# The first modulation woven into the convolution's products, the second layer's last gate summed a layer earlier, and bias tiles loaded beside its attention

## The chip, the cores and the metric

The kernel runs on one core of a Trainium2 chip. The core has five engines that run their own instruction streams: TensorE (PE in the profile, with its weight loads apart as PEld), VectorE (DVE), ScalarE (ACT), GpSimd (POOL) and SyncE (SP), which here issues all loads, one after the other, to the core's 16 DMA engines. The engines wait for each other only where an instruction needs something that another one makes, and each takes its instructions in the order in which they stand in its stream. The metric is the device time of one execution in microseconds, the median of several runs.

## The reference

Two models of two layers each run one after the other on 256 tokens of width 1024, all in 32-bit floats. The change touches the first model, whose layers mix a differential attention, a pooling and a convolution, then run an FFN. Six vectors per layer (`sh1` to `g2`, each 1024 wide) come from a product of a conditioning vector with `w_mod`, and they modulate the norms and gate the sums. The second model's dilated attention adds a bias by relative position.

```python
def adaln(cond, w_mod, b_mod):
    m = jnp.dot(jax.nn.silu(cond), w_mod) + b_mod
    return jnp.split(m[..., None, :], 6, axis=-1)

for l in range(DEPTH):                      # first model, DEPTH = 2
    sh1, sc1, g1, sh2, sc2, g2 = adaln(c, w_mod[l], b_mod[l])
    csh1, csc1, cg1, csh2, csc2, cg2 = adaln(c_ctx, w_mod[l], b_mod[l])
    h = modulate(rms_norm(x, norm1_g[l]), sh1, sc1)          # h * (1 + sc1) + sh1
    hc = modulate(rms_norm(xc, norm1_g[l]), csh1, csc1)
    q, k, v, up, ca, cb = project_inputs(h, w_in[l], ...)    # ca, cb: the convolution's inputs
    ...                                                      # the same for hc (context)
    mix = concatenate([attn, pool_o, conv_o])
    x = x + g1 * (mix @ w_out[l])
    x = x + g2 * swiglu(modulate(rms_norm(x, norm2_g[l]), sh2, sc2), w_ffn_in[l], w_ffn_out[l])
    ...                                                      # layer 0: the same for xc, 512 tokens in all

for l in range(DEPTH):                      # second model
    ...
    o_b = dilated_attention(q_d, k_d, v_d, rel_bias)         # s + bias[t5_bucket(rel)]
    x = x + mixed @ w_out[l]
    x = x + conv_ffn(rmsnorm(x, ffn_norm[l]), w_up[l], conv_w[l], conv_b[l], w_down[l])
```

## The kernel before

Every weight matrix is read from memory once, in pieces of 512 KB. A piece lands in a buffer `raw` (four of them), ScalarE casts it into the high half of a buffer `hl` (L202), VectorE subtracts to get the low half (L204), and a product of 32-bit accuracy is three TensorE matmuls: high with high, high with low, low with high (all through `mm`, L156). A load waits until the VectorE instruction that last read its `raw` buffer is done. All loads are issued by SP in program order (`dma`, L148). Outputs gather in PSUM banks named `acc`, `aux` and `ob`.

**The start** (`start()`). `x` and the context are loaded, normalized and turned by TensorE transposes (`turn`, copies at L768 and L770). The convolution's inputs need the modulated norm: `mod(c)` multiplies the conditioning vector with chunk `c` of `w_mod` (four chunks, buffers `wm` and `a`), and `products(c)` modulates two of the eight blocks of 128 columns of the normalized input, casts and subtracts them (L780, L781), and runs 24 matmuls of 128x512 on the convolution's weights. The program's order is `mod(0)`, `mod(1)`, `products(0)`, `mod(2)`, `products(1)` and so on. Between `products(2)` and `products(3)` SP gets many small loads (parameter `rows`, `gb`, `poolw`, `km`), and two transposes of `rows` (L309) follow all products on TensorE. Then the convolution's gate (`conv_gate`, L1204 and L1205) empties the banks, and `layer1` begins with the query projection (`qk_chunk`, `acc<-hl,a` 128x512).

**The weave.** `weave(main, side, rate)` runs two generators: at each step of the main one the side one is given `rate` steps, and what is left of the side at the end of the main runs after it. In layer 0 the FFN (`ffn_wide`, 512 tokens) is the main and `side2` the side, with rate 0.85. A step of `side2` is, for most of its length, one of `ada_sums`: a load of a `w_mod` block (128x1024) into `raw` and a multiply-add on VectorE (L353 for the first of eight, L355 for the other seven). After eight, `sums_to_gates` (or `sums_to_cols`) sums over partitions with a TensorE product (`aux<-s,ones`) and adds the result to the gate, which was loaded with `b_mod` (L398).

**Layer 1** (256 tokens, `layer1` with `l=1`). First the convolution's inputs (`conv_proj`, four pieces of `w_in`, 24 matmuls of 128x256 each), then query, key, pooling and values woven with the convolution's taps (L1236 on VectorE), then the attention woven with the output projection (`out_proj`, 96 matmuls of 128x512 in all), then the FFN (`ffn_narrow`, 256 tokens: per 256 hidden columns 96 matmuls `aux<-a,hl` 128x256 and 24 `acc<-hl,a` 128x512). The FFN is woven with `side3`: seven empty steps, the eight sums of part 5 of layer 1 (the gate `g2`), `dil_bias` (16 loads of `dbias`, 16x8x256 each, into two tiles for the second model), and `prepare2(0)`, the small loads for the second model's first layer. That model's FFN is woven with a side that has no sums.

The place of each instruction in its engine's stream follows from the program's order and a scheduler that fills in work that was put off (`later`, `flush`, `behind`).

## Time and profile before

| | |
|---|---|
| median of 3 runs | 1668.41 us (1668.08 to 1669.04) |
| the profiled execution | 1668.3 us, of which the span in the trace is 1666.5 us |
| TensorE busy | 1620.5 us, 97% of the span |
| VectorE, ScalarE, GpSimd busy | 1163.9, 793.5 and 40.9 us |
| mean granted TensorE clock | 0.986 of full speed |
| read from memory | 259.84 MB, 157 GB/s over the span |

All times below are microseconds from the start of the span. TensorE is busy nearly throughout, so what counts are the few stretches in which it waits or runs at a reduced clock, and what ends these waits. A busy time of TensorE is modelled from its matmuls' ends.

### The profile page before, as it was taken

Reading aid. Unit: us, or ns where it says so; the run is one execution under the profiler, and the core shown is the slowest. Engines: PE = TensorE matmul, PEld = TensorE weight load, DVE = VectorE, ACT = ScalarE, POOL = GpSimd, SP = SyncE. Lnnn points to the kernel's source line nnn. Section 1 sums busy time; section 2 is a strip of 40 time slices with the busy share of each in tenths; the row PEclk is TensorE's granted clock in tenths of the full one; section 3 lists DMA queues with packets and bytes.
Section 4 is the critical chain, followed back from the end, with each engine's and each line's share of the span. In section 5 each row is a group of like instructions: output and inputs, shape, how many; then the busy total and the mean of one; then the engine's idle time right before and its main releaser. Section 6 shows DMA issues by size and latency. Waiting matters only on the chain.

```text
span 1666.5 us, 24530 instructions
## 1 busy us (share of the span) xinstructions
PE 1620.5 (97%) x9401; PEld 1376.3 (83%) x9401; DVE 1163.9 (70%) x2074; ACT 793.5 (48%) x1339; POOL 40.9 (2%) x99
## 2 busy tenths in 40 slices
PE   7999989999999999999799899999999999999999
PEld 5787568878888888886799798888999888799998
DVE  4796656857575455977565558767887887678786
ACT  4334446323222224555543346755555576665553
POOL 1000000000000000000000001000000010000000
PEclk8999999999999999999899999999999999999999
DMA  9421651745375543532379655423656554246653
GB/s 329 127 91 56 244 181 56 238 150 167 110 233 169 174 149 103 152 112 76 110 224 250 181 184 166 137 88 117 193 187 190 168 161 146 74 130 190 190 181 123
DMA packets 183013, 262.75 MB, mean 158 GB/s; under 512 B 11277, under 2 KB 122864, under 8 KB 182896
## 3 DMA queue, kind: packets, MB, share of 16 engines
q1 hardware_dynamic: 182616, 260.85, 49.9%
q8 instruction: 74, 1.21, 0.3%
q10 hardware_dynamic: 280, 0.33, 0.2%
q14 instruction: 43, 0.35, 0.1%
HBM read 259.84 MB, written 1.31 MB: 157 GB/s over the span
## 4 chain that ended last, share of the span: by engine, by line
PE 83%; DVE 9%; issue 4%; ACT 3%; POOL 1%; DMA 1%; SPq 0%; ACTq 0%; POOLq 0%; DVEq 0%
PE aux L156 40%; PE acc L156 33%; PE ob L156 7%; PE aux L248 3%; DVE hl L204 2%; DVE a L1236 2%; DVE s L1236 1%; ACT hl L202 1%; DMA raw<-in_w_in_dram 1%; ACT s L461 1%; DVE sm L843 1%; POOL sm L163 0%; DVE s L852 0%; DVE a L862 0%; SPq L148 0%
## 5 line engine op out<-in xcount | busy, mean ns | idle before, releaser
L156 PE MATMUL acc<-hl,a 128*128 128x512 f32 (+3 forms) x3072 | 717.4, 387 | 8.3 <-ACT hl L202 2.9
L156 PEld LDWEIGHTS acc<-hl,a 128*128 128x128 f32 x3072 | 554.5, 190 | 117.6 <-ACT hl L202 4.7
L202 ACT CAST hl<-raw 128x1024 fp32r<-128x1024 f32 (+2 forms) x382 | 393.8, 1037 | 474.2 <-PE aux L156 151.2
L156 PE MATMUL aux<-a,hl 128*128 128x256 f32 (+1 forms) x4032 | 578.4, 304 | 4.7 <-ACT hl L202 1.6
L204 DVE TENSOR_TENSOR hl<-raw,hl 128x1024 fp32r<-128x1024 f32 (+2 forms) x382 | 457.3, 1201 | 166.5 <-ACT hl L202 164.5
L156 PEld LDWEIGHTS aux<-a,hl 128*128 128x128 f32 x4032 | 540.0, 192 | 37.4 <-ACT a L462 2.0
L355 DVE SCALAR_TENSOR_TENSOR s<-raw,csf,s 128x1024 f32<-128x1024 f32 x70 | 88.6, 1280 | 45.1 <-DMA raw<-in_w_mod_dram 45.0
L248 PEld LDWEIGHTS aux<-km,s 128*128 128x128 f32 (+1 forms) x416 | 48.9, 144 | 35.0 <-issue 17.6
L248 PE MATMUL aux<-km,s 128*128 128x128 f32 (+1 forms) x416 | 65.8, 283 | 11.9 <-DVE s L443 8.0
L156 PEld LDWEIGHTS ob<-a,s 128*128 128x128 f32 x416 | 52.1, 194 | 15.9 <-ACT s L1313 9.7
L156 PE MATMUL ob<-a,hl 128*128 128x512 f32 (+1 forms) x288 | 64.3, 372 | 0.0
L156 PE MATMUL ob<-a,s 128*128 128x64 f32 (+1 forms) x416 | 56.8, 281 | 2.4 <-ACT s L1313 1.7
L156 PEld LDWEIGHTS ob<-a,hl 128*128 128x128 f32 x288 | 51.2, 188 | 9.3
L524 ACT ACTIVATE s<-aux 128x512 f32<-128x512 f32 x33 | 19.7, 597 | 66.0 <-PE aux L156 66.0
L552 ACT ACTIVATE s<-s,c2a,c2b 128x256 f32<-128x256 f32 x88 | 47.9, 592 | 3.3 <-DVE s L549 3.2
L527 ACT CAST a<-s 128x512 fp32r<-128x512 f32 x33 | 20.4, 618 | 54.7 <-DVE s L526 54.6
L549 DVE TENSOR_TENSOR s<-aux,km 128x512 f32<-128x512 f32 x44 | 30.4, 690 | 20.7 <-PE aux L156 20.7
L1236 DVE SCALAR_TENSOR_TENSOR a<-up,c,a 128x512 f32<-128x512 f32 x60 | 43.3, 743 | 0.5
L248 PE MATMUL aux<-km,a 128*128 128x128 f32 (+1 forms) x196 | 31.9, 295 | 11.0 <-ACT a L770 7.1
L525 DVE SCALAR_TENSOR_TENSOR s<-s,aux 128x512 f32<-128x512 f32 x33 | 22.6, 684 | 28.0 <-ACT s L524 28.0
L409 ACT ACTIVATE jk<-a 128x512 bf16<-128x512 f32 x44 | 28.2, 641 | 26.3 <-DVE a L1023 19.9
L248 PEld LDWEIGHTS aux<-km,a 128*128 128x128 f32 (+1 forms) x196 | 24.0, 148 | 19.3 <-ACT a L770 7.5
(255 smaller groups left out, 1329.3 us busy)
## 6 DMA issues: line engine op xcount, KB each, us to landing
raw<-in_w_ffn_in_dram SPq DMA_DIRECT2D x88, 512.0 KB
raw<-in_w_up_dram SPq DMA_DIRECT2D x88, 512.0 KB
raw<-in_w_in_dram SPq DMA_DIRECT2D x60, 512.0 KB
raw<-in_w_mod_dram SPq DMA_DIRECT2D x56, 512.0 KB
raw<-in_w_ffn_out_dram SPq DMA_DIRECT2D x44, 512.0 KB
raw<-in_w_down_dram SPq DMA_DIRECT2D x44, 512.0 KB
wm<-in_w_mod_dram SPq DMA_DIRECT2D x16, 1024.0 KB
raw<-in_w_out_dram SPq DMA_DIRECT2D x32, 512.0 KB
```

What stands on the lines that cost most here:

```text
L156: self.nc.tensor.matmul(o, lhsT, rhs, start=start, stop=stop)
L202: nc.scalar.copy(hl[:, 0, :n], raw[:, :n])
L204: nc.vector.tensor_sub(hl[:, 1, :n], raw[:, :n], hl[:, 0, :n].bitcast(F32))
L248: self.nc.tensor.transpose(b[:rows, j * P:(j + 1) * P], s, self.ident)
L355: self.nc.vector.scalar_tensor_tensor(accs[s], raw, c, accs[s], op0=ALU.mult, op1=ALU.add)
L409: self.nc.scalar.activation(junk, x[:, h * 512:(h + 1) * 512], AF.Square, scale=D ** -0.5, accum_out=ss[:, h:h + 1])
L524: nc.scalar.activation(th, g, AF.Tanh, scale=0.5)
L525: nc.vector.scalar_tensor_tensor(th, th, 1.0, g, op0=ALU.add, op1=ALU.mult)
L527: nc.scalar.copy(hi, th)
L549: nc.vector.tensor_mul(y, x.rearrange("p (j t) -> p j t", j=2), R2)
L552: nc.scalar.activation(o[:, j, :], y[:, j, :], AF.Identity, scale=wc(1, ff), bias=bc(ff))
L1236: nc.vector.scalar_tensor_tensor(o, up[:, ct, :, k:k + SEQ], w, o, op0=ALU.mult, op1=ALU.add)
```

## The change

It has four parts. In `start()`, `mod(c+1)` now runs inside `products(c)`, after the first of its two blocks; the splits of the weights are held behind its copies, and the first splits of the query weights behind the last cast and subtraction. The sums of layer 1's part 5 move from `side3` to the end of `side2`, so into layer 0's FFN; the gate's load and `sums_to_gates` stand right after `conv_proj` in layer 1. The loads of `dil_bias` move from `side3` to the side of layer 1's attention, one step beside each step of the output projection. With these gone, `prepare2(0)` stands earlier in `side3`.

```diff
-    def split(self, raw, a, b, mark=None):
+    def split(self, raw, a, b, mark=None, first=None):
...
-        nc.scalar.copy(hl[:, 0, :n], raw[:, :n])
+        with self.behind(first):
+            nc.scalar.copy(hl[:, 0, :n], raw[:, :n])
...
-        def mod(c):
+        def mod(c, mark=None):
...
-                for k0 in (0, 4):
-                    self.ada_products(rb[:, o:o + 256], k0, raws[c, part][:, k0:k0 + 4, :])
-                nc.scalar.copy(r[:, o:o + 256], rb[:, o:o + 256])
+                with self.behind(mark):
+                    for k0 in (0, 4):
+                        self.ada_products(rb[:, o:o + 256], k0, raws[c, part][:, k0:k0 + 4, :])
+                copy = nc.scalar.copy(r[:, o:o + 256], rb[:, o:o + 256])
...
+            return end, copy
...
-                        self.mm(o, lo[:, j, w], hT[0][h][:, kk, :], start=False, stop=(k == KD - 1))
+                        mark = self.mm(o, lo[:, j, w], hT[0][h][:, kk, :], start=False, stop=(k == KD - 1))
+                if j == 0 and c < 3:
+                    ends = mod(c + 1, mark)
+            return ends if c < 3 else (sub, cast)
...
-        mod(0)
-        w_split(0)
+        w_split(0, mod(0))
         w_load(1)
         mod_load(2)
-        mod(1)
-        products(0)
-        w_split(1)
+        w_split(1, products(0))
...
-        products(3)
-        first = [self.split(raw, 2, 512) for raw in first]
+        ends = products(3)
+        first = [self.split(raw, 2, 512, *ends) for raw in first]
...
         if last:
+            g2 = [self.gate(l, 5, 0)]
+            self.sums_to_gates(g2)
             band = band_load()
...
                 yield from self.ada_sums(l + 1, 2, [0])
                 self.sums_to_gates([self.gate_next])
+                yield from self.ada_sums(l + 1, 5, [0])
...
-        self.weave(
-            self.diff_attention(S, qT, kT, v, rq, q_toks, mA, LAG), (next(out) for _ in range(4)), 0.5)
+        bias = []
+
+        def side():
+            tables = self.dil_bias(bias)
+            for _ in range(4):
+                next(out)
+                next(tables, None)
+                yield
+
+        self.weave(self.diff_attention(S, qT, kT, v, rq, q_toks, mA, LAG), side(), 0.5)
...
-        g2 = [self.gate(l, 5, 0)]
...
             for _ in range(7):
                 yield
-            yield from self.ada_sums(l, 5, [0])
-            self.sums_to_gates(g2)
-            yield from self.dil_bias(bias)
             nxt.append(self.prepare2(0))
```

**The order on the engines.** The following rows are the instruction streams before and after at three places; a row is line, operation, output and inputs (with buffer numbers), and shape. Lines after L153 are one to nine higher in the changed kernel.

At the boundary of layer 0 and layer 1, SP's stream before: the last `w_mod` blocks of `side2`, then the four pieces of `conv_proj`, then the first piece of the query weights.

```order
L148 DMA raw_5201<-in_w_mod_dram 128x1024
L148 DMA raw_5204<-in_w_mod_dram 128x1024
L148 DMA raw_5219<-in_w_in_dram 128x8x128
L148 DMA raw_5272<-in_w_in_dram 128x8x128
L148 DMA raw_5306<-in_w_in_dram 128x8x128
L148 DMA raw_5335<-in_w_in_dram 128x8x128
```

And after: eight more blocks of `w_mod` (5214 to 5235) stand ahead of them.

```order
L148 DMA raw_5201<-in_w_mod_dram 128x1024
L148 DMA raw_5204<-in_w_mod_dram 128x1024
L148 DMA raw_5214<-in_w_mod_dram 128x1024
L148 DMA raw_5217<-in_w_mod_dram 128x1024
L148 DMA raw_5220<-in_w_mod_dram 128x1024
L148 DMA raw_5223<-in_w_mod_dram 128x1024
L148 DMA raw_5226<-in_w_mod_dram 128x1024
L148 DMA raw_5229<-in_w_mod_dram 128x1024
L148 DMA raw_5232<-in_w_mod_dram 128x1024
L148 DMA raw_5235<-in_w_mod_dram 128x1024
L148 DMA raw_5244<-in_w_in_dram 128x8x128
L148 DMA raw_5297<-in_w_in_dram 128x8x128
```

The first convolution piece (5219 before, 5244 now) has moved behind eight loads of 512 KB that go through the same four `raw` buffers.

VectorE's stream at the same place, before: the last tile's steps of the norm, with the splits of the convolution's pieces (`hl`) between them.

```order
L204 TENSOR_TENSOR hl_5221<-raw_5219,hl_5221 128x1024
L1023 TENSOR_TENSOR a_401_2085<-a_401_2085,s_831_5162 128x512
L398 TENSOR_TENSOR gate_3277<-gate_3277,aux_5207 128x512
L204 TENSOR_TENSOR hl_5274<-raw_5272,hl_5274 128x1024
L463 TENSOR_TENSOR a_801_4992<-s_833_5170,a_799_4990 128x4x128
L398 TENSOR_TENSOR gate_3277<-gate_3277,aux_5210 128x512
L443 TENSOR_SCALAR s_836_5189<-a_401_2085,sm_5196 128x512
L463 TENSOR_TENSOR a_802_4993<-s_835_5182,a_800_4991 128x4x128
```

After: the eight sums stand behind the last tile's norm (L444, the former L443), and the first piece's split behind the sums.

```order
L444 TENSOR_SCALAR s_836_5189<-a_401_2085,sm_5196 128x512
L354 TENSOR_SCALAR s_846_5213<-raw_5214,csf 128x1024
L356 SCALAR_TENSOR_TENSOR s_846_5213<-raw_5217,csf,s_846_5213 128x1024
L464 TENSOR_TENSOR a_801_4992<-s_862_5278,a_799_4990 128x4x128
L356 SCALAR_TENSOR_TENSOR s_846_5213<-raw_5220,csf,s_846_5213 128x1024
L464 TENSOR_TENSOR a_802_4993<-s_864_5290,a_800_4991 128x4x128
L356 SCALAR_TENSOR_TENSOR s_846_5213<-raw_5223,csf,s_846_5213 128x1024
L356 SCALAR_TENSOR_TENSOR s_846_5213<-raw_5226,csf,s_846_5213 128x1024
L356 SCALAR_TENSOR_TENSOR s_846_5213<-raw_5229,csf,s_846_5213 128x1024
L356 SCALAR_TENSOR_TENSOR s_846_5213<-raw_5232,csf,s_846_5213 128x1024
L356 SCALAR_TENSOR_TENSOR s_846_5213<-raw_5235,csf,s_846_5213 128x1024
L205 TENSOR_TENSOR hl_5246<-raw_5244,hl_5246 128x1024
```

TensorE there, before: transposes of the norm (L248), one of the two products for the gate of part 2 (5207), then the convolution's products, with the last tile's transposes further behind.

```order
L248 MATMUL aux_5165<-km,s_825_5126 128x128 x4
L248 MATMUL aux_5177<-km,s_825_5126 128x128 x4
L156 MATMUL aux_5207<-s_759_4710,ones 128x512
L156 MATMUL acc_5217<-a_799_4990,hl_5221 128x256
L156 MATMUL acc_5217<-a_801_4992,hl_5221 128x256
L156 MATMUL acc_5217<-a_799_4990,hl_5221 128x256 x2
```

After: the product of the new sums (`aux_5397`) stands ahead of the first convolution product.

```order
L156 MATMUL aux_5207<-s_759_4710,ones 128x512
L156 MATMUL aux_5210<-s_759_4710,ones 128x512
L249 MATMUL aux_5273<-km,s_836_5189 128x128 x4
L249 MATMUL aux_5285<-km,s_836_5189 128x128 x4
L156 MATMUL aux_5397<-s_846_5213,ones 128x512
L156 MATMUL acc_5242<-a_799_4990,hl_5246 128x256
L156 MATMUL acc_5242<-a_801_4992,hl_5246 128x256
```

The products of the convolution, which filled TensorE between the transposes of the norm before, are now behind all of them and behind the sums.

At the end of the start, TensorE before: the last products of `products(3)`, the transposes of the parameter rows, and the query projection.

```order
L156 MATMUL acc_157<-a_15_150,hl_499 128x512
L156 MATMUL acc_157<-a_13_148,hl_499 128x512
L309 MATMUL aux_584<-km,rows_506 128x89
L309 MATMUL aux_588<-km,rows_520 128x48
L156 MATMUL acc_623<-hl_569,a_12_147 128x512 x2
L156 MATMUL acc_623<-hl_569,a_14_149 128x512
```

After: the transposes of the rows stand ahead of all of `products(3)` (weights `hl_499`).

```order
L156 MATMUL acc_157<-a_13_148,hl_434 128x512
L310 MATMUL aux_584<-km,rows_506 128x89
L310 MATMUL aux_588<-km,rows_520 128x48
L156 MATMUL acc_154<-a_13_148,hl_499 128x512
L156 MATMUL acc_155<-a_13_148,hl_499 128x512
L156 MATMUL acc_156<-a_13_148,hl_499 128x512
```

ScalarE before: the cast of the third piece of the query weights (`hl_682`) behind both of the convolution's gates (L1204).

```order
L202 CAST hl_572<-raw_504 128x1024
L780 CAST a_13_148<-a_11_146 128x512 x2
L1204 ACTIVATE s_84_578<-acc_156 128x512
L689 ACTIVATE sm_610<-sm_609 128x2
L1204 ACTIVATE s_85_581<-acc_157 128x512
L202 CAST hl_682<-raw_680 128x1024
```

After: it stands ahead of them (L1213).

```order
L203 CAST hl_569<-raw_502 128x1024
L203 CAST hl_572<-raw_504 128x1024
L203 CAST hl_682<-raw_680 128x1024
L1213 ACTIVATE s_84_578<-acc_156 128x512
L1213 ACTIVATE s_85_581<-acc_157 128x512
```

So `products(3)` now comes after the small loads of the rows, and the emptying of its banks after a load of 512 KB.

At the end of layer 1's attention, TensorE before: the last products of the attention (`ob`), and the output projection (`acc<-hl,a` 128x512), of which 60 matmuls stand ahead of these rows' end of the attention and 36 behind it.

```order
L156 MATMUL ob_6251<-a_927_5805,s_1052_6336 128x128 x4
L156 MATMUL ob_6251<-a_927_5805,s_1054_6347 128x128 x4
L248 MATMUL aux_6400<-km,s_1044_6302 128x128 x2
L156 MATMUL acc_6039<-hl_6375,a_954_5996 128x512 x6
L156 MATMUL acc_6040<-hl_6385,a_954_5996 128x512 x6
L248 MATMUL aux_6405<-km,s_1056_6354 128x128 x2
```

After: 36 stand ahead of it and 60 behind, as the rows of the first piece (`hl_6363`) now follow the last transposes of the attention.

```order
L156 MATMUL ob_6298<-a_939_5838,s_1068_6398 128x128 x4
L249 MATMUL aux_6451<-km,s_1058_6349 128x128 x2
L249 MATMUL aux_6456<-km,s_1070_6405 128x128 x2
L156 MATMUL acc_6072<-hl_6363,a_855_5238 128x512
L156 MATMUL acc_6073<-hl_6363,a_855_5238 128x512
L156 MATMUL acc_6074<-hl_6363,a_855_5238 128x512
L156 MATMUL acc_6075<-hl_6363,a_855_5238 128x512
```

So 24 matmuls, and the splits of their weights, have moved from beside the attention to behind it.


## Rows read from the trace of the kernel before

**Rows 1.** The page: busy time of TensorE, chain by engine, and the split's subtraction.

```profile
PE 1620.5 (97%) x9401; PEld 1376.3 (83%) x9401; DVE 1163.9 (70%) x2074; ACT 793.5 (48%) x1339; POOL 40.9 (2%) x99
...
PE 83%; DVE 9%; issue 4%; ACT 3%; POOL 1%; DMA 1%; SPq 0%; ACTq 0%; POOLq 0%; DVEq 0%
...
L204 DVE TENSOR_TENSOR hl<-raw,hl 128x1024 fp32r<-128x1024 f32 (+2 forms) x382 | 457.3, 1201 | 166.5 <-ACT hl L202 164.5
```

**Rows 2.** Windows: stretch, its length, busy us (instructions) per engine, TensorE clock, DMA share, GB/s.

```profile
20.00:42.00 22.00, 21.19 (x162) 14.23 (x162) 11.47 (x28) 8.20 (x15) 0.00 (x0) 0.90 1.05 348
...
680.00:700.00 20.00, 20.00 (x92) 16.47 (x91) 19.93 (x50) 7.91 (x10) 0.00 (x0) 1.00 0.51 156
...
740.00:800.00 60.00, 58.02 (x278) 39.41 (x277) 40.40 (x99) 35.63 (x73) 4.82 (x10) 1.00 0.23 74
...
900.00:920.00 20.00, 18.09 (x117) 15.61 (x115) 8.24 (x10) 5.81 (x7) 0.00 (x0) 1.00 1.07 239
...
920.00:940.00 20.00, 16.04 (x79) 13.91 (x80) 11.00 (x26) 7.28 (x9) 0.00 (x0) 0.83 0.49 141
```

**Rows 3.** Timeline of the start: start us, us, engine, line, operation [idle before <-releaser].

```profile
17.32 1.04 ACT L202 CAST hl<-raw 128x1024 fp32r<-128x1024 f32 x1 [5.55 <-DMA raw<-in_w_in_dram]
...
44.83 0.32 SPq L148 DMA_DIRECT2D rows<-in_b_mod_dram  x1
...
47.19 1.05 ACT L202 CAST hl<-raw 128x1024 fp32r<-128x1024 f32 x1 [1.86 <-DMA gb<-in_q_norm_g_dram]
...
51.55 3.71 SPq L148 DMA_DIRECT2D raw<-in_w_in_dram  x4
...
52.24 9.15 PE L156 MATMUL acc<-a,hl 128*128 128x512 f32 x39
...
61.59 4.60 PE L156 MATMUL acc<-hl,a 128*128 128x512 f32 x19
```

**Rows 4.** Timeline of SP at the layer boundary.

```profile
631.59 9.94 SPq L148 DMA_DIRECT2D raw<-in_w_in_dram  x4
```

**Rows 5.** Timeline of TensorE at the layer boundary.

```profile
664.11 1.60 PE L156 MATMUL acc<-a,hl 128*128 128x256 f32 x7
...
670.60 7.80 PE L156 MATMUL acc<-a,hl 128*128 128x256 f32 x63
...
678.23 6.99 PE L156 MATMUL acc<-hl,a 128*128 128x512 f32 x30
```

**Rows 6.** Timeline of VectorE at the layer boundary.

```profile
669.59 0.48 DVE L443 TENSOR_SCALAR s<-a,sm 128x512 f32<-128x512 f32 x1
```

**Rows 7.** Timelines of SP and VectorE: loads of w_mod and their first uses.

```profile
846.28 0.75 DVE L353 TENSOR_SCALAR s<-raw,csf 128x1024 f32<-128x1024 f32 x1 [1.47 <-DMA raw<-in_w_mod_dram]
...
848.19 0.34 SPq L148 DMA_DIRECT2D raw<-in_w_mod_dram  x1
...
852.95 1.28 DVE L355 SCALAR_TENSOR_TENSOR s<-raw,csf,s 128x1024 f32<-128x1024 f32 x1 [1.94 <-DMA raw<-in_w_mod_dram]
...
869.04 0.34 SPq L148 DMA_DIRECT2D raw<-in_w_mod_dram  x1
...
872.91 1.28 DVE L355 SCALAR_TENSOR_TENSOR s<-raw,csf,s 128x1024 f32<-128x1024 f32 x1 [1.03 <-DMA raw<-in_w_mod_dram]
```

**Rows 8.** A window of 4 us behind TensorE's longest idle stretch, columns as in rows 2.

```profile
812.00:816.00 4.00, 4.00 (x20) 4.00 (x20) 0.69 (x1) 0.86 (x2) 0.00 (x0) 0.50 0.02 6
```

**Rows 9.** Timeline of TensorE, from layer 1's attention to its FFN.

```profile
807.71 1.94 PE L248 MATMUL aux<-km,s 128*128 128x128 f32 x8 [6.32 <-DVE s L443]
...
811.24 4.08 PE L156 MATMUL aux<-a,hl 128*128 128x256 f32 x16 [1.60 <-ACT a L462]
...
1001.87 4.43 PE L156 MATMUL acc<-hl,a 128*128 128x512 f32 x18
```

**Rows 10.** Timeline of TensorE: the FFN that follows, its first products and its last pair.

```profile
1148.02 0.39 PE L156 MATMUL aux<-a,hl 128*128 128x256 f32 x1
...
1325.72 4.50 PE L156 MATMUL acc<-hl,a 128*128 128x512 f32 x19
```

More of the change, by code (lines that the diff above doesn't have):

```diff
@@ L155, in mm @@
     def mm(self, o, lhsT, rhs, start=True, stop=True):
-        self.nc.tensor.matmul(o, lhsT, rhs, start=start, stop=stop)
+        return self.nc.tensor.matmul(o, lhsT, rhs, start=start, stop=stop)
     def rstd(self, ss, n, inv_d):
@@ L757, in mod @@
                     cols[:, k:k + 1].to_broadcast([P, 2]), op0=ALU.add, op1=ALU.mult)
-                nc.vector.tensor_scalar(Sv[:, :, k], o[:, 2:4], cols[:, KD + k:KD + k + 1], None, op0=ALU.add)
+                end = nc.vector.tensor_scalar(Sv[:, :, k], o[:, 2:4], cols[:, KD + k:KD + k + 1], None, op0=ALU.add)
+            return end, copy
         def turn():
@@ L769, in turn @@
                     else:
-                        nc.scalar.copy(dst, b)
+                        end = nc.scalar.copy(dst, b)
+            return end
         def products(c):
@@ L792, in w_load, with w_split @@
             ws[c] = self.load(self.wview(io["w_in"][0], 2 * c, 2, 1792, 2304), 2, 512)
-        def w_split(c):
-            ws[c] = self.split(ws[c], 2, 512)
+        def w_split(c, marks):
+            ws[c] = self.split(ws[c], 2, 512, *marks)
         for t in range(4):
@@ L1120, in side3 @@
             nxt[0].rest()
-        bias, nxt, end = [], [], {}
+        nxt, end = [], {}
         done = self.norm2(xin, lambda: nxt[0].cols("an", KD), end)
```

12 lines of the change are left out of this document (4 added, 8 removed).

## The prediction

> **What bounds the kernel now.** I read the page first. TensorE is busy 97% of the span, and the chain that ended last runs through it for 83% of its length [rows 1]. So the reader should not look for a slow engine but for the few places where TensorE waits, and ask of each part of the change what it does to one of them. The table by windows finds these places [rows 2]. In the start, from 20 to 42, the DMA engines are full (share 1.05, 348 GB/s): the program waits for its first weights, and no reordering of the arithmetic can be faster than they come. From 900 to 940, in the middle of layer 1's FFN, TensorE is busy 18.09 and 16.04 of 20 and its clock falls to 0.83: a hole in a stage that is otherwise full. Around the boundary of the layers, on the contrary, nothing is free: from 680 to 700 TensorE is busy 20.00 and VectorE 19.93 of 20. Then I read the timelines of the four places that the change touches, engine by engine [rows 3 to 7], and the orders of both kernels side by side, which show where an instruction now stands behind another.
>
> **The boundary: the moved sums.** The eight sums were put at the end of the side of layer 0's FFN. Their loads and additions are the last steps of that side, and the order shows that none of them finds a place beside the FFN: on VectorE they stand behind the last tile's norm, on SP the convolution's weights stand behind their loads, and on TensorE their product (`aux_5397`) stands ahead of the first convolution matmul. That is a chain on an engine that had no gap.
>
> Before, SP issued the four convolution pieces from 631.59 on [rows 4], 32 us ahead of the first product at 664.11; the query projection followed at 678.23 [rows 5]. After, these four slots go to the first four blocks of `w_mod`, which then lie in the four `raw` buffers until VectorE uses them. VectorE's step ahead of the sums begins at 669.59 and takes 0.48 [rows 6], so the sums begin at about 670.0. The first (no addition) takes 0.75, each other 1.28 [rows 7], some 1.2 of it before the next begins; two steps of the norm on half as many elements, an estimated 0.7 each, stand between the first ones. So the eight take at least 0.75 + 7 x 1.2 + 1.4 = 10.5 of VectorE's time, without any wait for a load, and end no sooner than 680.5. The loads add a little: blocks 5 to 8 are issued as buffers come free, the eighth after the fourth sum, at 675.9. From issue to first use a block takes 3.9 (869.04 to 872.91) to 4.8 us (848.19 to 852.95) [rows 7]; I take 3.9, since few loads are on the way, so it lands at 679.8 and its sum ends at 681.1. The first convolution piece can only be issued once the fifth block's buffer is free, at 677.1, lands at 681.0, and is cast (1.04 [rows 3]) and subtracted (1.2 [rows 1]): 683.4. The 96 products of the convolution lasted from 664.11 to 678.23 before, with transposes between; alone they take 96 x 0.124 (63 in 7.80 [rows 5]), about 12, so the query projection begins at 695 instead of 678.2: **17 us later**.
>
> The page DMA: Bandwidth & Descriptors of the Trainium skill (section Anatomy of one DMA) gives a fixed 2.0 us plus the bytes at 436 GB/s for loads issued from GpSimd; for 512 KB that would be an estimate of 3.2 us. By it the eighth block and the piece would land some 0.7 us sooner, and the stall would be that much shorter. The loads here are issued from SP and the rows show more, so the sum keeps the rows' figure.
>
> TensorE also loses its clock. It is idle from about 671 to 681. The nearest row is the kernel's longest idle stretch, 6.32 before 807.71 [rows 9]: after it the granted clock was still 0.50, 1.2 of the 2.4 GHz, from 812 to 816, with TensorE busy for all of these 4 us [rows 8], so at least 2 were lost. I take 2 here, bounds 0 and 3.5 (twice the stretch, less the part before TensorE had work). **Sum at the boundary: +19.** From below: 15.5 (sums back to back, no clock lost). From above: 22 (loads at 4.8, clock as at 808, and two more additions to a gate, some 0.7 each, on a VectorE that is full from 680 to 700). For these two additions by themselves I add 0.5 to the sum. Nothing later gives this back: the projections that follow keep TensorE full.
>
> **The FFN of layer 1: what the removal gives.** From the first product at 811.24 to the last pair of the same form at 1001.87 the stage takes 190.6 [rows 9]. The FFN after it, with the same shapes and a side without sums and bias tiles, takes 1325.72 - 1148.02 = 177.7 [rows 10]. So at most 13.0 can be won. The start at half clock after 807.71 [rows 8] stays. TensorE's idle time in the hole is 20 - 18.09 + 20 - 16.04 = 5.9 [rows 2]; the lowered clock in it, 0.83 over 16 busy us, is some 2.7; the product of the sums is at most four matmuls of 128x512, 1.0. Together **-10**, bounds 8 and 13. The tiles' 16 loads and the small loads that followed them on SP's queue made the hole; the small loads stay, but earlier and without the tiles ahead of them.
>
> **The start.** Two gains are real: the cast that held ScalarE until the weights had landed (idle 5.55 until 17.32 [rows 3]) no longer stands ahead of the transposes' copies, and TensorE works on the products while later chunks land. But until about 42 the DMA engines set the pace, and then the order puts the transposes of the rows, which need the last `rows` load, ahead of `products(3)`. SP issues that load at 44.83, and the `gb` load right behind it was waited for until 47.19 [rows 3]. So these 24 matmuls start at about 47.3 and take 24 x 0.235 (39 in 9.15 [rows 3]) = 5.6, until 53. Then ScalarE has the cast of the third query piece ahead of the gate that empties the banks: issued at 51.55 [rows 3], landing after 3.9 and cast in 1.04, with the gate behind it, it makes about 57.2, where the query projection was at 61.59. That is 4.4 gained; the waits of some 4 us ahead of 47 and again ahead of 57 cost clock, for which I take 1.4 (less than half the price after the 6.32). **-3**, bounds 0 and -5.
>
> **The attention of layer 1.** The tiles' loads go at no cost: from 740 to 800 the DMA engines are used at a share of 0.23 [rows 2]; without that cover they would hold the loads of the output projection behind them on SP, and cost what they cost in the FFN, up to 6. What does count is that 24 matmuls of the output projection, and the splits of their weights, have moved behind the attention, where 36 stood before, as the order shows. If the attention is paced by its softmax, its length stays and the tail grows by 24 x 0.24 = 5.8, or 7 with a late split. If it is paced by TensorE, it shrinks by as much, and by up to 4 more if the splits on ScalarE and VectorE paced it. I take the middle of 0 and 5.8, **+3**.
>
> **Sum:** the profiled execution's own 1668.3 (1.8 of it around the span, 0.1 under the median) + 19 + 0.5 - 10 - 3 + 3 = 1677.8 us.
>
> **The rivals.**
> *The small loads hold nothing at the start, and the kernel is not slower.* One place: `products(3)`. All its data have landed by about 42. If the rows also land by then, the 24 matmuls and the last modulation end at about 50, and if the third query piece is cast in time, the query projection starts between 50 and 52 instead of 57: a gain of 9.6 to 11.5 in place of 3, and 1669.3 to 1671.2. It decides from a gain of 9.2 on (1671.6). For it: TensorE has work for 8 us only after 42. Against it: SP's own rows at 44.83 and 51.55, which come behind a full DMA queue in both kernels. 0.13.
> *The boundary stays at its lower bound, and the FFN gets the whole 13.* 1668.3 + 15.5 + 0.5 - 13 - 3 + 3 = 1671.3, or 1668 with an attention that loses nothing. For it: the second model's FFN does run in 177.7, small loads and all. Against it: the half clock after 807.71 comes from the wait ahead of the FFN, which stays. 0.12.
> *More goes wrong behind the attention.* The splits of four pieces in a row, ScalarE ahead of VectorE, hold the 60 matmuls, the idle stretch ahead of the FFN grows with them, and the start gives nothing: 1668.3 + 21 + 0.5 - 9 + 7 = 1688. For it: 60 products need all four pieces after the last exponential. 0.13.
> *The sums do not wait at the boundary at all,* as the change has it, because they run beside layer 0's FFN: then -10 - 3 + 3 = 1658 to 1661. The order speaks flatly against it. 0.04.
>
> **How the numbers follow.** The forecast (boundary 15.5 to 22, FFN 8 to 11, start 0 to -5, attention 0 to 6) has the remaining 0.58 and runs from 1672 to 1685. A difference of 0.2%, 3.3 us, is about what a measurement of this kernel can tell from none, so faster is below 1665.1 and slower above 1671.7. Slower: the forecast, the third rival, and a few parts of the first two, 0.75. Same: most of the first two, 0.16. Faster: the fourth and the best cases of the first two, 0.09. The range takes in the first rival's end below and most of the third: 1667 to 1687.
>
> **What would show it.** Right: TensorE idle about 10 us shortly before 682 on VectorE's sums, then on the split of the first convolution piece, and the query projection at about 693 (start 3 earlier, boundary 17 to 19 later). Eight loads of `w_mod` of which the last four are issued after 670. FFN 1 in about 180 from its first product to its last pair, no hole at 110 us after its start. `products(3)` waiting for `rows` until about 47. The stretch between the attention's last `ob` and the FFN some 6 longer. Wrong: additions of the sums beside layer 0's last FFN products; a query projection before 52; a hole that stays in the FFN because the small loads alone made it (then 6 more is lost).

## The result

The changed kernel takes 1693.99 us (median of 4 runs, 1691.03 to 1702.2) against 1668.72 (4 runs): a ratio of 1.0152, 95% interval 1.013 to 1.0174, so 1.5% slower. The profiled execution took 1694.32, its span is 1692.5, 26.0 more than before. The first two rows of the page are to be read against those of [rows 1]: TensorE's busy time grew by 9 us, and its share of the chain fell from 83% to 78%.

```profile
PE 1629.3 (96%) x9401; PEld 1379.0 (81%) x9401; DVE 1168.1 (69%) x2074; ACT 795.8 (47%) x1339; POOL 41.1 (2%) x99
...
PE 78%; DVE 11%; issue 4%; ACT 3%; DMA 2%; POOL 1%; SPq 0%; ACTq 0%; POOLq 0%; DVEq 0%
```

The windows that answer to [rows 2] show where: from 20 to 42 TensorE does less than before (16.84 of 22 instead of 21.19) though the DMA engines are as full; from 680 to 700, where nothing was free, it is busy for only half the time, at a granted clock of 0.59; and the hole of the FFN is gone. That FFN begins 38.7 later now, so what was 900 to 940 is now 938.7 to 978.7, and TensorE is busy there throughout.

```profile
20.00:42.00 22.00, 16.84 (x108) 11.36 (x108) 9.11 (x22) 5.86 (x10) 0.00 (x0) 0.83 1.05 347
...
680.00:700.00 20.00, 9.98 (x51) 8.29 (x52) 13.93 (x13) 5.44 (x7) 0.00 (x0) 0.59 0.98 306
...
938.70:958.70 20.00, 20.00 (x148) 19.04 (x147) 11.01 (x11) 8.50 (x10) 0.00 (x0) 1.00 0.60 179
...
958.70:978.70 20.00, 20.00 (x140) 18.70 (x140) 11.38 (x12) 8.87 (x10) 0.00 (x0) 1.00 0.61 192
```

Landmarks in TensorE's timeline, in us from the start of each span, give the account. The column "behind" is how far the changed kernel has fallen behind by then; the last one says which stretch cost it, and how much.

| | before | after | behind | stretch |
|---|---|---|---|---|
| query projection of layer 0 begins | 61.59 | 65.86 | 4.3 | start +4.3 |
| last run of products in layer 0's FFN | 657.21 | 664.20 | 7.0 | layer 0 +2.7 |
| query projection of layer 1 | 678.23 | 706.13 | 27.9 | boundary +20.9 |
| first attention product | 749.02 | 777.75 | 28.7 | +0.8 |
| FFN of layer 1, first product | 811.24 | 849.96 | 38.7 | attention's tail +10.0 |
| its last pair | 1001.87 | 1027.77 | 25.9 | FFN -12.8 |

**The boundary.** The timelines of SP, VectorE, ScalarE and TensorE in the changed kernel, to be read against [rows 4 to 6]. Ten `w_mod` blocks go ahead of the convolution's pieces; the sums begin at 676.92, the eighth waits 0.91 for its load and ends at 689.5; TensorE waits 11.32 for it; the first piece lands at 690.36, 5.7 after its issue.

```profile
631.81 51.84 SPq L148 DMA_DIRECT2D raw<-in_w_mod_dram  x10
...
684.64 5.46 SPq L148 DMA_DIRECT2D raw<-in_w_in_dram  x4
...
676.92 0.75 DVE L354 TENSOR_SCALAR s<-raw,csf 128x1024 f32<-128x1024 f32 x1
...
688.22 1.28 DVE L356 SCALAR_TENSOR_TENSOR s<-raw,csf,s 128x1024 f32<-128x1024 f32 x1 [0.91 <-DMA raw<-in_w_mod_dram]
...
690.36 1.04 ACT L203 CAST hl<-raw 128x1024 fp32r<-128x1024 f32 x1 [9.07 <-DMA raw<-in_w_in_dram]
...
676.06 2.18 PE L249 MATMUL aux<-km,s 128*128 128x128 f32 x8 [2.97 <-DVE s L444]
...
689.56 2.08 PE L156 MATMUL aux<-s,ones 128*128 128x512 f32 x2 [11.32 <-DVE s L356]
...
706.13 4.23 PE L156 MATMUL acc<-hl,a 128*128 128x512 f32 x16
```

**The start,** by the changed kernel's timelines of TensorE, with the last chunk's steps on VectorE and ScalarE (L205 is the held subtraction of a split, L784 the scaling, L785 the cast). The first twelve products take 5.08, at a granted clock of 0.56 behind an idle 2.55; then each chunk waits once, 1.50, 1.51 and 1.25 for a cast, with 10.6 from chunk to chunk. The transposes of the rows (L310) wait for nothing. The last two rows are of the kernel before: its first product, and its window from 42 to 62 (columns as in [rows 2]), in which TensorE was busy throughout.

```profile
26.27 5.08 PE L156 MATMUL acc<-a,hl 128*128 128x512 f32 x12 [2.55 <-ACT a L785]
...
38.93 3.00 PE L156 MATMUL acc<-a,hl 128*128 128x512 f32 x12 [1.50 <-ACT a L785]
...
49.52 3.00 PE L156 MATMUL acc<-a,hl 128*128 128x512 f32 x12 [1.51 <-ACT a L785]
...
58.43 0.43 PE L310 MATMUL aux<-km,rows 89*128 89x89 f32 x2
...
60.12 5.74 PE L156 MATMUL acc<-a,hl 128*128 128x512 f32 x24 [1.25 <-ACT a L785]
...
65.86 2.34 PE L156 MATMUL acc<-hl,a 128*128 128x512 f32 x9
...
57.87 1.22 DVE L205 TENSOR_TENSOR hl<-raw,hl 128x1024 fp32r<-128x1024 f32 x1
...
59.00 1.05 DVE L784 TENSOR_SCALAR a<-a,G,S 128x256 f32<-128x256 f32 x3
...
59.45 1.27 ACT L785 CAST a<-a 128x512 fp32r<-128x512 f32 x2 [2.63 <-DVE a L784]
...
32.64 1.20 PE L156 MATMUL acc<-a,hl 128*128 128x512 f32 x4
...
42.00:62.00 20.00, 20.00 (x117) 15.15 (x116) 11.13 (x27) 7.34 (x13) 0.20 (x1) 1.00 0.41 137
```

**The attention's tail and the FFN,** by TensorE's timeline of the changed kernel, against [rows 9]. 55 products stand in one run behind the attention, after a wait of 3.02; the two waits for the norm (6.32 and 1.60) stay as they were. The last two rows are of the kernel before: twelve products stand there where TensorE now waits 3.02, and only 0.27 of waiting is left. The FFN takes 1027.77 - 849.96 = 177.8, what the second model's took in [rows 10].

```profile
822.42 0.48 PE L249 MATMUL aux<-km,s 128*128 128x128 f32 x2 [3.02 <-DVE s L1338]
...
822.58 14.35 PE L156 MATMUL acc<-hl,a 128*128 128x512 f32 x55
...
846.42 1.94 PE L249 MATMUL aux<-km,s 128*128 128x128 f32 x8 [6.32 <-DVE s L444]
...
849.96 2.37 PE L156 MATMUL aux<-a,hl 128*128 128x256 f32 x8 [1.60 <-ACT a L463]
...
1027.77 2.55 PE L156 MATMUL acc<-hl,a 128*128 128x512 f32 x10
...
790.26 2.99 PE L156 MATMUL acc<-hl,a 128*128 128x512 f32 x12
...
793.52 0.41 PE L248 MATMUL aux<-km,s 128*128 128x128 f32 x2 [0.27 <-DVE s L1329]
```

### The profile page after: what moved, and what is told of

It reads as the page before. It is cut to its first block, busy times and chain, and to the rows that moved or that the text cites. A ratio compares the mean times of both kernels' runs of the same rounds, so it can differ in the third digit from the quotient of the medians.

```text
span 1692.5 us, 24523 instructions
## 1 busy us (share of the span) xinstructions
PE 1629.3 (96%) x9401; PEld 1379.0 (81%) x9401; DVE 1168.1 (69%) x2074; ACT 795.8 (47%) x1339; POOL 41.1 (2%) x99
## 4 chain that ended last, share of the span: by engine, by line
PE 78%; DVE 11%; issue 4%; ACT 3%; DMA 2%; POOL 1%; SPq 0%; ACTq 0%; POOLq 0%; DVEq 0%
PE aux L156 38%; PE acc L156 30%; PE ob L156 7%; PE aux L249 3%; DVE hl L205 2%; DVE a L1245 2%; DVE s L1245 1%; DMA raw<-in_w_in_dram 1%; DVE s L356 1%; ACT s L462 1%; DMA raw<-in_w_mod_dram 1%; ACT hl L203 1%; ACT jk L410 1%; POOL sm L163 0%; DVE sm L845 0%
## 5 line engine op out<-in xcount | busy, mean ns | idle before, releaser
L205 DVE TENSOR_TENSOR hl<-raw,hl 128x1024 fp32r<-128x1024 f32 (+2 forms) x382 | 458.5, 1203 | 175.2 <-ACT hl L203 173.3
L156 PE MATMUL acc<-a,hl 128*128 128x512 f32 (+1 forms) x192 | 42.1, 372 | 7.3 <-ACT a L785 6.8
L550 DVE TENSOR_TENSOR s<-aux,km 128x512 f32<-128x512 f32 x44 | 30.4, 691 | 20.9 <-PE aux L156 20.9
L156 PEld LDWEIGHTS acc<-a,hl 128*128 128x128 f32 x192 | 31.8, 212 | 14.5 <-ACT a L785 7.9
L556 DVE SCALAR_TENSOR_TENSOR s<-s,c2b,s 128x255 f32<-128x255 f32 x88 | 38.6, 479 | 0.1
```

The source lines that it names most:

```text
L156: return self.nc.tensor.matmul(o, lhsT, rhs, start=start, stop=stop)
L205: nc.vector.tensor_sub(hl[:, 1, :n], raw[:, :n], hl[:, 0, :n].bitcast(F32))
L550: nc.vector.tensor_mul(y, x.rearrange("p (j t) -> p j t", j=2), R2)
L556: nc.vector.scalar_tensor_tensor(o[:, j, 0:SEQ - 1], y[:, j, 1:SEQ], wc(2, ff), o[:, j, 0:SEQ - 1], op0=ALU.mult, op1=ALU.add)
```

## The experiments

Times are medians; the runs of one group share a chip and its runs of the kernel before (1668.85 with the first four, 1669.01 with the next, 1669.56 with the third, 1669.82 with the last).

**The three parts, one by one.** Each of the first three makes one part of the diff above on the kernel before: `e1_start` the hunks of `split`, `mod` and `products`, `e2_sums` and `e3_tables` these:

```diff
# e2_sums
+                yield from self.ada_sums(l + 1, 5, [0])
...
+            g2 = [self.gate(l, 5, 0)]
+            self.sums_to_gates(g2)
...
-            yield from self.ada_sums(l, 5, [0])
-            self.sums_to_gates(g2)
# e3_tables
+                next(out)
+                next(tables, None)
...
-            yield from self.dil_bias(bias)
```

`e8_tables_behind` is the changed kernel with

```diff
             for _ in range(4):
                 next(out)
-                next(tables, None)
                 yield
...
         for _ in out:
             pass
         self.flush()
+        for _ in self.dil_bias(bias):
+            pass
```

> The kernel before with the start's part of the change alone (modulation woven into the products, splits held behind it); sums and tables stay in layer 1's FFN. Theory: this part alone costs what the changed trace shows at its end, because it lays TensorE's products out as one chain per chunk (products, modulation, gate, split, scaling, cast) with 1.5 us idle in each: query projection at 65.9 instead of 61.6, so +4.3, and with the 2.7 that layer 0 adds until its end +7: 1673 to 1676. Rival: the start is only late because of loads that belong to the other parts or to noise of the shared queue; then it is within 1 us of before, 1668 to 1669.

> The kernel before with the sums' part of the change alone (the eight sums at the end of layer 0's side, tables still in layer 1's FFN). Theory: the boundary costs 21 whatever the start does, and the FFN gets back only the sums' share of its hole, 2 to 6 of the 12.7, since the tables' loads stay: 1683 to 1688. Rival: the hole in the FFN was made by sums and tables together and goes when either goes, so 12 come back: 1677 to 1678. Second rival: the boundary was long only because the start had shifted it against the loads; then no more than 10 there and 1666 to 1676.

> The kernel before with the tables' part alone (loads of the bias tiles beside the attention, sums still in layer 1's FFN). Theory: 24 matmuls of the output projection move behind the attention and cost 10 there; the FFN gets back the tables' share of its hole, 7 to 11: 1667 to 1672. Rival: the tail's 10 come from the late boundary (buffers, clock) and not from the tables; then the tail stays at 21.0 from the last ob to the FFN and the time is 1658 to 1661.

> The changed kernel, but with the tables' 16 loads issued behind all loads of the output projection instead of between them; its stream has 60 matmuls beside the attention and 36 behind again. Theory: the tail returns to some 21 us, 10 less than in the changed kernel, and the FFN keeps most of its gain: 1683 to 1687. Rival: the order of the loads does not matter and the longer tail comes from late weights; then 1692 to 1695. Third case: the tables now collide with the FFN's first weights and up to 6 of the 10 are lost: 1687 to 1690.

| | us | ratio to before (95%) |
|---|---|---|
| e1_start | 1671.42 | 1.0018 (1.0007 to 1.0029) |
| e2_sums | 1696.15 | 1.0153 (1.0137 to 1.017) |
| e3_tables | 1669.81 | 1.0004 (0.9994 to 1.0013) |
| e8_tables_behind | 1682.63 | 1.0081 (1.0064 to 1.0099) |

With the start alone the query projection begins at 65.94, 4.3 late, and the median is 2.6 higher; the +7 that I expected did not come, since layer 0's 2.7 is not the start's. The boundary does not need the start: TensorE's timeline of `e2_sums` has the same wait for the additions, 11.66. But nothing came back in the FFN: 836.00 to 1029.23 is 193.2, more than the 190.6 of before, and the time is above all that was expected.

```profile
685.20 2.08 PE L156 MATMUL aux<-s,ones 128*128 128x512 f32 x2 [11.66 <-DVE s L355]
...
836.00 4.29 PE L156 MATMUL aux<-a,hl 128*128 128x256 f32 x17 [1.60 <-ACT a L462]
...
1029.23 5.12 PE L156 MATMUL acc<-hl,a 128*128 128x512 f32 x21
```

In `e3_tables`, the same view, the tail is there without any late boundary (55 products behind a wait of 3.16), and the FFN runs in 1004.58 - 824.59 = 180.0 with the sums in it, 10.6 less than before. So nearly all of the hole was the tables'.

```profile
797.05 0.41 PE L248 MATMUL aux<-km,s 128*128 128x128 f32 x2 [3.16 <-DVE s L1336]
...
797.22 14.34 PE L156 MATMUL acc<-hl,a 128*128 128x512 f32 x55
...
824.59 3.65 PE L156 MATMUL aux<-a,hl 128*128 128x256 f32 x14 [1.60 <-ACT a L462]
...
1004.58 5.73 PE L156 MATMUL acc<-hl,a 128*128 128x512 f32 x24
```

In `e8_tables_behind`, where 36 products stand behind the attention again, the tail is back at 22.0 from the start of the last `ob`; a wait of 4.26 for the FFN's first weights is new, and the one of 6.32 is down to 4.54.

```profile
831.69 1.94 PE L249 MATMUL aux<-km,s 128*128 128x128 f32 x8 [4.54 <-DVE s L444]
...
837.89 0.80 PE L156 MATMUL aux<-a,hl 128*128 128x256 f32 x2 [4.26 <-ACT hl L203]
```

**Each suspect by itself.** `e5_sums_rate` is `e2_sums` with another rate, `e6b_split_free` is `e1_start` with the later splits not held, `e7_turn_first` is before with the first cast behind `turn`'s copies:

```diff
# e5_sums_rate
-                side2(), 0.85)
+                side2(), 1.0)
# e6b_split_free
-            ws[c] = self.split(ws[c], 2, 512, *marks)
+            ws[c] = self.split(ws[c], 2, 512, *(marks if c == 0 else ()))
# e7_turn_first
-        turn()
+        end = turn()
         mod(0)
-        w_split(0)
+        w_split(0, end)
```

`e10_behind_alone` is before with the tables' loads behind `out`, as in `e8_tables_behind`.

> The sums' part alone, as in e2_sums, but the weave of layer 0's FFN gives its side 1.0 steps per step instead of 0.85, so that all eight sums stand beside FFN products in the streams. Theory: the 21 at the boundary were only the sums' place behind the FFN's end; they go (convolution's products at 664 to 668), the FFN of layer 1 still has its hole, made by the tables: 1668 to 1673. Rival: the sums cost about the same wherever they stand, since eight more loads go through the four raw buffers that the FFN's weights need: 10 or more spread over layer 0's FFN, 1679 or more.

> The start's part alone, as in e1_start, but the splits of the convolution's weights from the second chunk on are not held behind the modulation, so VectorE's subtraction of a split stands ahead of the scalings' chain. Theory: the held subtraction (1.22) is in the chain of each of three chunks; without it the query projection starts at 62 to 63 instead of 65.9, and the time falls by 1 to 3 against e1_start, 1668.5 to 1670.5. Rival: the chunks are paced by TensorE's own order (modulation products between the halves) and the wait moves to another link; query projection still after 65, 1670.5 to 1672.5.

> The kernel before with one edit: the cast of the first convolution weights on ScalarE held behind the last copy of the turned input, all else in the old order (modulations ahead of products). Theory: the transposes end some 5 us sooner as in the changed kernel, but from there TensorE's work, 29 us of modulations and products, sets the end, and it can begin only as its data come: the query projection starts 1 to 5 sooner, at 57 to 60.5, and the time is 1664 to 1668. Rival: the loads alone set the start; the query projection stays within 1 of 61.6 and the time within 1 of before.

> The kernel before with one edit: the tables' loads moved from the FFN's side to behind the output projection's loads; start and sums as before, sums still in layer 1's FFN. Theory: the hole in the FFN was made by the tables' loads alone, and here they disturb nothing: 10 to 12 less, 1657 to 1660. Rival: it takes both, sums and tables, to be gone; then 3 to 6 less, 1663 to 1666.

| | us | ratio to before (95%) |
|---|---|---|
| e5_sums_rate | 1680.21 | 1.0064 (1.0047 to 1.008) |
| e6b_split_free | 1673.68 | 1.003 (1.002 to 1.004) |
| e7_turn_first | 1673.17 | 1.0021 (1.0011 to 1.003) |
| e10_behind_alone | 1660.45 | 0.9944 (0.9929 to 0.9959) |

In `e5_sums_rate` the boundary pays nothing, but layer 0's FFN takes 8 longer, so the rival holds for most of it; the new rate moves all steps of the side, so these 8 are not the sums' alone. In `e6b_split_free`, by TensorE's timeline, the wait per chunk falls from 1.5 to 0.38, as the theory has it, and the query projection begins at 64.30: 1.6 sooner, not 3. What is left is 9.5 per chunk, nearly all of it TensorE's own work. The median is no better than that of `e1_start` all the same.

```profile
39.52 3.04 PE L156 MATMUL acc<-a,hl 128*128 128x512 f32 x12 [0.38 <-ACT a L785]
...
64.30 5.98 PE L156 MATMUL acc<-hl,a 128*128 128x512 f32 x25
```

In `e7_turn_first`, the same view, the first product is no earlier than before (32.88); TensorE waits 2.86 for a copy that stands behind a cast of weights not yet landed, and then its first 23 products take 7.44, 0.32 each. Its query projection begins at 63.71, and the time is above both expectations.

```profile
26.07 0.38 PE L156 MATMUL ob<-km,s 128*128 128x2 f32 x2 [2.86 <-ACT s L750]
...
34.18 7.44 PE L156 MATMUL acc<-a,hl 128*128 128x512 f32 x23
```

`e10_behind_alone` is the one edit that pays; with the sums still there its FFN takes 990.63 - 810.39 = 180.2 by TensorE's timeline.

```profile
810.39 0.80 PE L156 MATMUL aux<-a,hl 128*128 128x256 f32 x2 [4.26 <-ACT hl L202]
...
990.63 5.76 PE L156 MATMUL acc<-hl,a 128*128 128x512 f32 x24
```

**Doses.** These runs give more or less of one cause. `e9_tables_before` is the changed kernel with all of `dil_bias` ahead of the attention's weave, `e12_late_sums` is `e10_behind_alone` with the sums' part and a denser side late in the stage, `e14_half_out` is `e2_sums` with rate 0.92, which leaves five sums behind the FFN's end in the program's order:

```diff
# e9_tables_before
+        for _ in self.dil_bias(bias):
+            pass
         def side():
...
-                next(tables, None)
# e12_late_sums
-        for _ in main:
-            due += rate
+        for i, _ in enumerate(main):
+            due += 1.25 if rate == 0.85 and i >= 36 else rate
# e14_half_out
-                side2(), 0.85)
+                side2(), 0.92)
```

`e16_copies_first` holds the first two casts behind the first two modulations' copies:

```diff
-        w_split(0)
+        w_split(0, mod(0))
...
-        w_split(1)
+        w_split(1, copy)
```

> The changed kernel, but with all 16 loads of the tables issued ahead of the output projection's loads; its stream has none of that projection's 96 matmuls beside the attention and all 96 behind. Theory: what counts is how many stand behind (36 gave 21 us from the last ob to the FFN, 60 gave 31); 96 give 31 + 36 x 0.24 = 39.7 or a little more, so the time is 6 to 10 above the changed kernel's, unless the attention itself runs faster without them: 1694 to 1704. Rival: the tail grew by the tables' traffic or a late weight, not by the count; here all weights lie ready, the tail stays at 31 or falls, and the time is 1690 to 1694.

> Start as before; tables behind the output projection's loads; sums in layer 0's FFN with the side's rate 0.85 for 36 steps and 1.25 after, so that all eight stand beside FFN products and the FFN's first pieces see the old rate. Theory: of the 8 that e5 paid in layer 0's FFN, the 5 at its beginning and the 3 near 430 came from the denser side and go; the boundary pays nothing, the narrow FFN runs in 178: 1655 to 1659, up to 3 under e10. Rival: sums cost in layer 0's FFN what they cost in layer 1's, or more; 1660 to 1666.

> The sums' part alone at rate 0.92: three sums beside the FFN, five behind its end. Theory: the stall at the boundary is VectorE's additions and the loads that wait for a raw buffer; with five blocks (four of them in buffers) it shrinks from 21 to 11 to 15, so qk1 stands 11 to 15 behind the end of layer 0 more than before; with the tables' hole and up to 5 in layer 0's FFN: 1680 to 1690. Rival: the stall is a fixed price for any sum behind the FFN's end (queue order on SP and TensorE): again 19 or more, 1690 to 1697.

> The kernel before with two casts of the start held back on ScalarE (the first convolution weights behind the first modulation's copy, the second behind the second's), all else in the old order. Theory: e7 lost 2 at the query projection because the cast of the second weights stood ahead of a copy that the modulation needed (TensorE idle 2.86 at 26.07); with it gone the first product starts before 30 and the query projection at 57 to 61, 1664 to 1669. Rival: TensorE's early work only leaves it idle later while the loads come, at half clock; then the query projection is again at 61.5 to 64, 1668.5 to 1673.

| | us | ratio to before (95%) |
|---|---|---|
| e9_tables_before | 1702.55 | 1.0199 (1.0183 to 1.0214) |
| e12_late_sums | 1669.48 | 1.0 (0.999 to 1.001) |
| e14_half_out | 1676.0 | 1.0042 (1.003 to 1.0055) |
| e16_copies_first | 1672.6 | 1.002 (1.0007 to 1.0033) |

The tail follows the count: from the start of the last `ob` to the FFN 21.2, 31.1 and 42.3 us with 36, 60 and 96 products behind. The attention itself, from its first product to the last `ob`, takes 41.0, 41.2 and 39.9, so taking all products out of it buys 1. The rows are TensorE's in `e9_tables_before`: the attention's first and last products, and the FFN's first.

```profile
774.30 1.98 PE L156 MATMUL aux<-a,a 64*128 64x512 f32 x6
...
812.43 2.05 PE L156 MATMUL ob<-a,s 128*128 128x128 f32 x16 [0.65 <-DVE sm L1332]
...
856.50 5.79 PE L156 MATMUL aux<-a,hl 128*128 128x256 f32 x24 [1.60 <-ACT a L463]
```

`e12_late_sums` went against both its expectations: layer 0's FFN takes 9.8 longer than before, only later in the stage than in `e5_sums_rate`. `e16_copies_first` goes the rival's way: with the copies free TensorE waits 3.71 for the second modulation's load instead. And `e14_half_out` contradicts both its theories. With the loads of five sums ahead of the convolution's pieces on the same queue, the boundary costs nothing (15.6 from the end of layer 0's last products to the query projection, 15.3 before), as its timelines of SP, VectorE and TensorE show:

```profile
624.03 13.14 SPq L148 DMA_DIRECT2D raw<-in_w_mod_dram  x5
...
639.23 5.30 SPq L148 DMA_DIRECT2D raw<-in_w_in_dram  x4
...
633.20 1.28 DVE L355 SCALAR_TENSOR_TENSOR s<-raw,csf,s 128x1024 f32<-128x1024 f32 x1
...
664.59 0.72 PE L156 MATMUL acc<-a,hl 128*128 128x256 f32 x4
...
679.55 17.16 PE L156 MATMUL acc<-hl,a 128*128 128x512 f32 x73
```

These five sums run from 628 to 643, beside the FFN's last products. Two things differ from the changed kernel: five are left and not eight, and their accumulator exists already. In the changed kernel the eight sums open a new one, from the pool of three that the norm's tiles come from (`S4`).

**The accumulator, and what moving the sums is worth.** `e17_own_acc` is the changed kernel with

```diff
-        accs = {s: self.S4([P, D]) for s in streams}
+        new = (lambda: self.A8([P, 2, D])[:, 0, :]) if own else (lambda: self.S4([P, D]))
+        accs = {s: new() for s in streams}
```

for the moved sums. `e19_half_behind` is `e14_half_out` with the tables behind `out`, and `e20_behind_again` is `e10_behind_alone` once more.

> The changed kernel, with the new sums' accumulator in a buffer of the big pool instead of the pool of three that the norm's tiles use; its stream has the eight sums between the steps of the last two tiles' norm instead of behind the last one, loads and queue order as in the changed kernel. Theory: the position of the sums, and so most of the 21 at the boundary, came from waiting for a buffer of that pool; the sums now begin some 12 us sooner, with the convolution's first split right behind the seventh: 4 to 10 left of the 21, 1677 to 1683. Rival: the stall comes from the loads (eight blocks through four buffers, and the convolution's pieces behind them), which are unchanged: 17 or more left, 1690 to 1694.

> Start as before; tables behind the output projection's loads; sums in layer 0 at rate 0.92, which cost nothing at the boundary in e14. If moving the sums is worth anything, it is here: the narrow FFN without sums and tables runs in 178 and the boundary is free, 1656 to 1660. Rival: what the denser side costs in layer 0's FFN eats that, and it stays above e10: 1661 to 1668.

> The same code as e10_behind_alone, for a closer interval beside e19 on one chip: the kernel before with the tables' loads behind the output projection's. Theory: 8 to 11 less than before, 1658 to 1661, and not slower than any version that moves the sums. Rival: e10's gain was partly the luck of layer 0, then 1661 to 1665.

| | us | ratio to before (95%) |
|---|---|---|
| e17_own_acc | 1681.63 | 1.008 (1.0063 to 1.0098) |
| e19_half_behind | 1664.86 | 0.9974 (0.9964 to 0.9984) |
| e20_behind_again | 1659.7 | 0.9946 (0.9933 to 0.9958) |

With a buffer of the big pool the first sum starts at 659.73 instead of 676.92, and the kernel is 12.4 faster than the changed one. Of that, 3.9 had come by layer 0's last products (660.34 instead of 664.20), which the edit does not touch. From the end of these products to the query projection it is 27.3, where the changed kernel has 36.2 and before 15.3: 9 of the 21 were the buffer's, and 12 stay. This lies between the two expectations for the boundary. That loads and additions alone make the 12 is not shown: SP's next load still waits 15.8 for that first sum (29.2 in the changed kernel), and what keeps the sum there no run tells. The rows are from its timelines of VectorE and TensorE.

```profile
659.73 0.75 DVE L355 TENSOR_SCALAR a<-raw,csf 128x1024 f32<-128x1024 f32 x1
...
660.34 5.73 PE L156 MATMUL acc<-hl,a 128*128 128x512 f32 x24
...
674.83 0.80 PE L156 MATMUL acc<-a,hl 128*128 128x256 f32 x2 [3.62 <-ACT hl L203]
...
693.36 16.52 PE L156 MATMUL acc<-hl,a 128*128 128x512 f32 x72
```

`e19_half_behind` stays 5 above `e20_behind_again`, so of the versions tried here the best leaves the sums where they were.

## Why the prediction was wrong

The direction and its main cause were right, the size was not: +9.5 was forecast, +25.3 came, outside the range. The profiled execution is 16 behind the sum; the start makes 7.3 of that and the attention 7.0, layer 0 2.7 and the boundary 1.4, and the FFN gives 2.8 back. By the prediction's own steps:

- **Boundary, +19 and 0.5: right, +20.9.** The chain went link by link as worked out, some 7 later, which is how late layer 0 ended: the eighth sum's end at 689.5 (681.1 worked out), the first piece issued at 684.64 (677.1), and it landed after 5.7 where I had taken 3.9. By the fit that the Trainium skill (DMA: Bandwidth & Descriptors, Anatomy of one DMA) gives for loads issued from GpSimd it was an estimate of 3.2; for this load, issued from SP with three more pieces on the way behind it, the row shows 5.7. But why the sums stood there was not said: I read it as a matter of the weave and the queue, and `e17_own_acc` shows that for 9 of the 21 it was the accumulator's buffer; the rest is open.
- **FFN, -10: too small, -12.8,** the upper bound of 13. The term took the idle time and the lost clock of the hole (8.6) for the loads of the tiles and of the rows, and only 1.0 for the sums. The four cases measure it: 190.6 with both, 193.2 with the tables alone, 180.0 with the sums alone, 177.8 with neither. So beside each other the tables cost 10.6 and the sums some 2.3, and without the sums the tables cost 15.4, more than both together. Why that is so no run shows.
- **Attention, +3: the first step that failed, +10.0.** I took the middle between an attention paced by TensorE and one paced by its softmax. `e9_tables_before` shows the second: the attention does not shrink. So the 24 products cost their full length, 24 x 0.26 = 6.2, and TensorE waits 3.0 ahead of them, where before twelve products filled that gap but for 0.27; my bound of 7 left that wait out. `e8_tables_behind` gives all of it back.
- **Start, -3: the wrong sign, +4.3 in the profile,** +2.6 in the median of `e1_start`. The step that failed is that `products(3)` waits for the `rows` load and that all before it is done when the loads are. The transposes of the rows waited for nothing. TensorE's own work set the end, and it had hardly a gap to fill: before, it was busy 21.19 of the 22 up to 42 and all of the 20 up to 62. By the timeline the products started 6.4 sooner (26.27 for 32.64), but then had the second modulation (3.2) between them instead of ahead, three waits for a cast (4.3), and their first twelve at a granted clock of 0.56 (some 2.2), together 9.7 of the 10.6 that were lost from there on. I had priced a lost clock at the waits near 47 and 57, where the granted clock stayed at 1.00, and not at 26, behind the gap that the weaving itself opens. My rival for the start assumed only 8 us of work after 42; TensorE was busy for 21 of the 24 that it took.
- **Layer 0, +2.7, had no term** and, as far as these profiles tell, is not the change's: see the last section.

The rivals: none came true as told. The third, slower by the attention's tail, named the right place, but with a smaller gain in the FFN than came and a start that gives nothing instead of a loss. The first had its condition right, since the row at 58.43 waits for nothing, but not its gain: the query projection came at 65.86 and not between 50 and 52. The second had the FFN right and the boundary wrong. The fourth is refuted by the wait at 689.56.

Parts and whole agree: 2.6 + 27.3 + 1.0 from the three parts alone, less the 4.8 by which the FFN gains more with both gone (12.8) than the two parts show (-2.6 and 10.6), makes 26.1 beside the 25.3 measured. Left open is what denser side steps cost layer 0's FFN, and why: 8.3 in `e5_sums_rate` and 9.8 in `e12_late_sums`, and at the one rate of 0.92 it was 3.2 in the profile of `e14_half_out` but 9.2 in that of `e19_half_behind`. In the traces TensorE waits there for others: 2.88 for a cast of weights in the first, 2.31, 1.33 and 2.15 for VectorE in the second, and 3.92 for VectorE in the last, after which the granted clock was 0.52 for 5.5 us.

## What to carry to other kernels

When work is moved into the cover of another stage, look first at what it must allocate there: here a new accumulator from a pool that the stage's end also uses put the work behind that end, though its first loads stood ahead. Small loads put between big ones can move arithmetic that a scheduler places by its loads: count the matmuls on either side of the covered stage in both orders, and price those that moved out at their full length if the stage is paced by another engine. And before weaving a chain into the engine that is the bound, add up that engine's own work from the first product on: here a start 6.4 sooner bought nothing, since it only opened gaps later. The version to keep is the smallest: the tables' loads behind the output projection's, 1659.7 us.

## What the runs showed that I had not expected

The stretch from layer 0's query projection to its FFN takes different times though no edit touches it: 219.2 us before, 221.7 and 221.8 in `e2_sums` and `e3_tables`, 218.0 in `e14_half_out` and 223.2 in `e19_half_behind`. The changed kernel has 221.5, and `e1_start`, with the same start, 217.1. TensorE's mean granted clock over the stretch goes with the time: 0.97 in the two shortest, 0.96 before, 0.95 in the three between 221.5 and 221.8, and 0.93 in the longest. Why the clock differs there from one execution to the next is open. So a difference of 5 us between two single profiles may lie there alone, and only medians of several runs tell such parts apart.
